# Opening by channel tiles and the end by halves of the tokens, in a two-layer decoder trunk

## The chip, the cores and the metric

The kernel runs on one core of a Trainium2 chip. TensorE (PE) multiplies matrices into PSUM banks, VectorE (DVE), ScalarE (ACT) and GpSimd (POOL) do the elementwise work, and the queues of SyncE (SP), ACT and POOL issue the DMA transfers. The metric is the device time of one execution in microseconds (us), lower is better. A profile is one execution with every instruction timed; its span is the time from the first to the last event on the core.

## The reference

One sequence of 256 tokens, 2048 channels, all in float32, two layers. Each layer has a token mixer and an MLP, and each of these is preceded by an RMSNorm with scale and shift computed from a vector `c` and followed by a gated residual:

```
mod = (silu(c) @ w_mod[i] + b_mod[i]);  sh1, sc1, g1, sh2, sc2, g2 = split(mod, 6)
u = rmsnorm(h, norm_mix_g[i]) * (1 + sc1) + sh1
h = h + g1 * mixer(u)          # layer 0: conformer convolution, layer 1: Mamba-2
u = rmsnorm(h, norm_mlp_g[i]) * (1 + sc2) + sh2
h = h + g2 * ((relu(u @ w1[i]) ** 2) @ w2[i])
return rmsnorm(h, final_norm_g)
```

The convolution mixer is `u @ w_pw1` (2048 to 4096 columns), a gated linear unit (GLU), a causal depthwise convolution of width 31, a LayerNorm with swish, and a second matrix. The Mamba-2 mixer projects to `z, x, B, C, dt`, convolves x, B and C over 4 positions, and scans over two chunks of 128 tokens in 8 groups of 8 heads: inside a chunk `(C B^T * decay) x`, across the chunks `C state * exp(acum)`, where `acum` is the running sum of `dt * A` in a chunk and `A = -exp(a_log)`. It ends with `y * silu(z)`, an RMSNorm per group, and an output matrix. The kernel must return the whole trunk's output.

## The kernel before

Activations lie with channels on partitions: `h[g]` holds four channel tiles of 128 channels by 256 tokens. Weights are read from HBM once each, in tiles of 1 MB (128 x 2048 float32). Large products split each weight tile into a high and a low half (`wh`, `wl`) by a cast on ACT and a difference on DVE, three or fewer products each; the first matrix of the convolution mixer is multiplied as it is.

*Modulation.* One segment (scale, shift, gate) of one channel tile is a product of a 1 MB tile of `w_mod` with `silu(c)`, held on all partitions in `scb`: one DVE instruction (L309) that also sums. `gemv` issues the load and this product, `mod_done` adds the bias and, for a scale, turns it into `(1 + scale) * norm gain`. The tiles rotate through four buffers `hid` and two `wm`. Modulation that is not needed at once is queued in `jobs` and pumped in between the weight tiles of later stages.

*The opening.* `conformer` squares x on ACT (L605, 16 instructions), sums over channels by 16 products with ones (L609), takes the root (L611). `native` then multiplies the first four blocks of 512 columns (`FIRST = 4`) of the first matrix; they fill all eight PSUM banks. It goes by groups of four channel tiles: all eight modulation products of group 0, the reciprocal of the root among them (L796), then four times a factor and a shift (`vectors`, L631 on DVE, L634 on ACT) to make `u[0]`; then for each group 0 to 2 and each block i a weight tile of 1 MB (512 rows by 512 columns) and its products (L760), with two modulation products of the next group behind each block. In group 3 the products go in three parts, two channel tiles, one and one, over all blocks. `glu` takes a block's banks when the last channel tile is in. After this, `native` is called once for each of the blocks 4 to 7, with the depthwise convolution of finished channel tiles on ACT, DVE and (for eight of the tiles) PE in between, and queued modulation.

All the small parameters are one tensor `par`, 1186 columns of 128 partitions, loaded at the start on ACT's queue. The tap weights of the PE convolution (`quad`) are loaded on POOL's queue. Weights and modulation tiles are loaded on SP's queue in program order (`stream`, L364); an issue waits there until its buffer is free.

*The second mixer.* `scores` and `scan` are generators: a step of theirs is taken between products of the projection (`step`), strictly one generator after the other, and `lag(n)` lets n steps pass. For each group `scores` loads the broadcast decays (`ac_d`, two `acc` tiles, on POOL's queue), adds the mask, takes exponentials; `scan` makes the state and adds the part from outside the chunk: a tile `e2` of the factors `exp(acum)` is loaded from `eac_d` (L1335, POOL's queue) and multiplied by `C state` (L1341). `gated` multiplies by the gate (L1363), squares (L1365), adds up (L1366, L1367) and sums over channels on PE (L558 in `rstd_cols`), for the root and reciprocal.

*The end.* The last MLP works with tokens on partitions: `ht[q]` holds the 128 tokens of half q by 2048 channels. `block_t` multiplies a block of 512 output columns for both halves, alternating between them, and the second half's products end a few instructions after the first's. `into_rows` multiplies the bank by the gate row (L1101), adds it to `ht` (L1105), squares with a sum (L1106), and multiplies by the final gain (L1107). `run` then adds the four sums of each half (L1406), takes root and reciprocal for both halves (L1407, L1408), scales (L1413 on ACT, L1415 on DVE) and stores four pieces of 512 KB (L1416).

The order on each engine is set by a list scheduler from the program order, the priorities (`high_priority`) and the explicit `issue_after`; SP's loads keep program order.

## Time and profile before

| | |
|---|---|
| median of the runs | 2562.72 us (2562.64 to 2563.96) |
| profiled execution | 2561.61 us, span 2559.8 us |
| PE busy | 2518.8 us |
| first product of the opening | 36.54 us |
| block 4 begins | 152.04 us |
| last product begins | 2547.57 us |
| loads and stores | 664.85 MB, mean 260 GB/s |

The profiled execution is 1.1 us below the median; its time lies 1.8 us above its span. In the rows of the profile, a line such as L760 is one of the kernel before, an operand `u,w` names tiles without their numbers, and a matmul of full float32 shows as two records each of its loads and its products. The idle time of an engine matters only where the end waits for it.

### The profile page before, as it was taken

What the parts mean: (1) busy time and instruction counts of PE and PEld (TensorE: products, weight loads), DVE (VectorE), ACT (ScalarE), POOL (GpSimd) and SP (SyncE); (2) the same over time, 40 slices, a digit from 0 to 9 for tenths busy, and PEclk for the clock granted to TensorE, in tenths of its full rate; (3) what the DMA queues carried; (4) which work ended last, traced back from release to release, by engine and by line L of the source; (5) the groups of instructions that cost most, each with busy time, mean ns of one, the idle gap of its engine ahead of it and who ended that gap; (6) DMA issues with size and microseconds to landing.
All of it is one profiled execution on the core that took longest, in us unless ns stands there. A gap on an engine that the chain in (4) does not pass through costs nothing. (4 is left out here: it accounts for less than half of the span.)

```text
span 2559.8 us, 36983 instructions
## 1 busy us (share of the span) xinstructions
PE 2518.8 (98%) x14707; PEld 2175.6 (85%) x14707; DVE 1916.5 (75%) x2467; ACT 1312.7 (51%) x2011; POOL 146.9 (6%) x212
## 2 busy tenths in 40 slices
PE   6999999999999999999999999999999999999998
PEld 5888799988888888888888888888998888888886
DVE  6679688878879878888777778898975565565565
ACT  2068454544434434448677777744454443443443
POOL 0011000000000000001000000000001101001000
PEclk8999999999999999999999999999999999999999
DMA  9998789688888878856555455688765555555553
GB/s 404 381 326 305 286 341 361 258 333 316 310 334 315 326 291 342 322 216 227 194 186 177 169 193 193 243 310 313 311 247 190 190 195 186 193 192 189 195 187 142
DMA packets 94895, 664.85 MB, mean 260 GB/s; under 512 B 10977, under 2 KB 10977, under 8 KB 16769
## 3 DMA queue, kind: packets, MB, share of 16 engines
q1 hardware_dynamic: 89138, 643.87, 68.0%
q0 software_dynamic: 5152, 16.97, 2.3%
q8 instruction: 115, 1.88, 0.3%
q10 hardware_dynamic: 432, 1.66, 0.2%
q14 instruction: 58, 0.48, 0.1%
HBM read 657.02 MB, written 2.20 MB: 258 GB/s over the span
## 5 line engine op out<-in xcount | busy, mean ns | idle before, releaser
L380 DVE TENSOR_TENSOR wl<-w,wh 128x1024 fp32r<-128x1024 f32 x768 | 940.9, 1229 | 472.6 <-ACT wh L378 468.2
L378 ACT CAST wh<-w 128x1024 fp32r<-128x1024 f32 x768 | 808.2, 1053 | 935.4 <-PE mm L409 478.5
L409 PE MATMUL mm<-u,wh 128*128 128x512 f32 x3136 | 994.2, 398 | 0.2 <-ACT wh L378 0.2
L409 PEld LDWEIGHTS mm<-u,wl 128*128 128x128 f32 x3136 | 587.7, 188 | 138.6 <-DVE wl L380 1.1
L409 PE MATMUL mm<-u,wl 128*128 128x256 f32 x3136 | 617.9, 278 | 0.7 <-DVE wl L380 0.7
L409 PEld LDWEIGHTS mm<-u,wh 128*128 128x128 f32 x3136 | 479.9, 189 | 7.7 <-issue 4.2
L462 PE MATMUL mm<-wh,hid 128*128 128x512 f32 x896 | 350.7, 391 | 0.0
L464 PE MATMUL mm<-wh,hid 128*128 128x512 f32 x896 | 348.7, 389 | 0.0
L463 PE MATMUL mm<-wl,hid 128*128 128x512 f32 x896 | 348.6, 389 | 0.0
L309 DVE SCALAR_TENSOR_TENSOR wm<-wm,scb 128x2048 f32<-128x2048 f32 x133 | 303.9, 2285 | 17.9 <-DMA wm<-wmT 17.9
L393 PE MATMUL mm<-u,wh 128*128 128x256 f32 x1408 | 254.7, 284 | 0.9 <-DVE u L523 0.6
L393 PEld LDWEIGHTS mm<-u,wh 128*128 128x128 f32 x1408 | 219.2, 192 | 4.0 <-ACT u L519 1.3
L760 PE MATMUL mm<-u,w 128*128 128x256 f32 x864 | 191.9, 383 | 20.4 <-ACT u L634 20.4
L760 PEld LDWEIGHTS mm<-u,w 128*128 128x128 f32 x864 | 164.6, 192 | 46.9 <-ACT u L634 21.6
L393 PE MATMUL mm<-u,wl 128*128 128x256 f32 x704 | 198.0, 283 | 0.6 <-DVE wl L380 0.6
L462 PEld LDWEIGHTS mm<-wh,hid 128*128 128x128 f32 x896 | 168.2, 188 | 35.6 <-issue 1.0
L464 PEld LDWEIGHTS mm<-wh,hid 128*128 128x128 f32 x896 | 168.2, 188 | 35.4
L463 PEld LDWEIGHTS mm<-wl,hid 128*128 128x128 f32 x896 | 168.2, 188 | 35.0 <-issue 0.5
L409 PE MATMUL mm<-hid,wh 128*128 128x512 f32 x448 | 141.9, 398 | 0.3 <-DVE lo L511 0.3
L309 DVE SCALAR_TENSOR_TENSOR hid<-hid,scb 128x2048 f32<-128x2048 f32 x47 | 107.3, 2286 | 40.8 <-DMA hid<-wmT 40.7
L393 PEld LDWEIGHTS mm<-u,wl 128*128 128x128 f32 x704 | 134.6, 192 | 0.8 <-DVE wl L380 0.8
L409 PEld LDWEIGHTS mm<-hid,wl 128*128 128x128 f32 x448 | 84.2, 188 | 19.8
(263 smaller groups left out, 1967.7 us busy)
## 6 DMA issues: line engine op xcount, KB each, us to landing
w<-w SPq DMA_DIRECT2D x256, 1024.0 KB, 4.9
wm<-wmT SPq DMA_DIRECT2D x138, 1024.0 KB, 7.1
w<-win SPq DMA_DIRECT2D x80, 1024.0 KB, 4.9
hid<-wmT SPq DMA_DIRECT2D x54, 1024.0 KB, 10.9
w<-pw SPq DMA_DIRECT2D x46, 1024.0 KB, 7.3
w<-wout SPq DMA_DIRECT2D x32, 1024.0 KB, 7.0
acc<-ac_d POOLq DMA_DIRECT2D x16, 512.0 KB, 7.2
xpad<-u POOLq DMA_DIRECT2D x24, 131.5 KB, 8.2
```

The lines of the kernel that those rows point to most:

```text
L309: self.sum = nc.vector.scalar_tensor_tensor(out=w, in0=w, scalar=1.0, in1=self.scb, op0=ALU.mult, op1=ALU.mult, accum_out=m[:, i:i + 1]).ins
L378: nc.scalar.copy(out=wh, in_=w[:, s, :])
L380: nc.vector.tensor_tensor(out=wl, in0=w[:, s, :], in1=wh.bitcast(F32), op=ALU.subtract)
L393: self.pe = self.nc.tensor.matmul(out, lhsT=lhsT, rhs=rhs, skip_group_check=True, **kw).ins
L409: self.pe = self.nc.tensor.matmul(out, lhsT=lhsT, rhs=rhs, start=start and not lows, stop=stop and bool(lows), skip_group_check=True).ins
L462: mm(banks[q], lhsT=hi, rhs=wh[:, k, :], start=g == 0 and t == 0, stop=False)
L463: mm(banks[q], lhsT=hi, rhs=wl[:, k, :], start=False, stop=False)
L464: mm(banks[q], lhsT=lo, rhs=wh[:, k, :], start=False, stop=g == 3 and t == 3)
L760: self.pe = nc.tensor.matmul(o, lhsT=w[:, t, j * P:(j + 1) * P], rhs=u[g][:, t, :], start=g == 0 and t == 0 and j < 2, stop=g == 3 and t == 3,
```

## The change

*Opening by channel tiles.* The first four blocks' weights become an array `open` of their own, arranged by channel tile: one 1 MB tile has the 128 rows of one channel tile for all four blocks (128 x 4 x 512). A new function `opening` goes through the 16 channel tiles: scale product, factor, shift product, `u` of this tile, then 16 products for all four blocks. Bias and gain of each single column are added on DVE (one, the shift of tile 14, on POOL). The squares of x are taken as three 128x1024 instructions and four small ones, added on DVE, and summed by 6 products instead of 16. 16 products that only fill PE's time stand between these sums and the first channel tile (`FILL[0]` was 0). Of `par` only the first 272 columns are loaded at the start, the rest behind the last `open` tile on SP's queue; the first `quad` load is held until the shift of tile 14 is made. `native` keeps blocks 4 to 7. The exponential for `A` (`na`) is held until the last square before the second mixer.

*End by halves.* In the very last block of `block_t` the products of the last six channel tiles are held and then issued for the first half of the tokens and after it for the second. `finish(q)` ends each half on its own: the sums of the first three blocks are added early, root and reciprocal, the last block times gain and reciprocal in one instruction, the rest scaled on DVE and ACT, two stores.

*Second mixer.* `e2` gets a place of its own in `par` (the columns of the depthwise taps, no longer needed), and its load is issued at the start of `scan`. `lag` before group 0's mask is 5 steps and not 3; after the last addition of `scan` 1 step and not 2; in `gated` 3 steps and not 2 (4 for group 0, as before).

```diff
-FILL = 0, 3, 5, 6, 8
+FILL = 16, 3, 5, 6, 8
...
+        "open": np.ascontiguousarray(pw1[:, :FIRST * 512].reshape(NT, P, FIRST, 512)),
...
-        nc.scalar.dma_start(out=self.par, in_=a["par"])
+        nc.scalar.dma_start(out=self.par[:, :SOON], in_=a["par"][:, :SOON])
...
-        if (layer, seg, kg) in ((0, SC1, 3), (0, SH1, 3)):
-            nc.vector.tensor_add(m, m, b)
+        if layer == 0 and seg in (SC1, SH1):
+            late = (seg, 4 * kg + i0) == (SH1, NT - 2)
+            self.closed = (nc.gpsimd if late else nc.vector).tensor_tensor(out=m, in0=m, in1=b, op=ALU.add).ins
...
+                held += [(4 * g + 2 * i + k, wh, wl, k) for k in range(2)]
+                if by_half and (g == 2 and i == 1 or g == 3 and i == 0):
+                    continue
+                order = [(q, *v) for q in range(2) for v in held] if g == 3 and i == 1 else [
+                    (q, *v) for v in held for q in range(2)]
+                for v in order:
+                    three(*v)
+                held = []
...
+        def opening(done):
...
+            self.turn_over(banks[0][0][:, :P], FILL[0], self.pe)
+            for ct in range(NT):
+                g, t = divmod(ct, 4)
+                self.gemv(0, SC1, ct, ((t, t + 1),))
+                if ct == 0:
+                    self.gemv(0, SH1, ct, ((t, t + 1),))
+                    with self.tc.issue_after(self.sum):
+                        nc.vector.reciprocal(r, r)
+                m = self.t("nrm", [P, T], bufs=2)
+                nc.vector.scalar_tensor_tensor(
+                    out=m, in0=self.h[g][:, t, :], scalar=self.mod_tile(0, SC1, g)[:, t:t + 1],
+                    in1=r, op0=ALU.mult, op1=ALU.mult)
+                if ct:
+                    self.gemv(0, SH1, ct, ((t, t + 1),))
+                if ct == NT - 2:
+                    self.after_open = self.closed
+                nc.scalar.activation(out=u[g][:, t, :], in_=m, func=AF.Identity,
+                                     bias=self.mod_tile(0, SH1, g)[:, t:t + 1])
+                w = self.load_w(a["open"][ct])
+                for i in range(FIRST):
+                    for j in range(4) if ct < NT - 1 else (0, 2, 1, 3):
+                        o = banks[i][j % 2][:, (j // 2) * T:(j // 2 + 1) * T]
+                        self.pe = nc.tensor.matmul(o, lhsT=w[:, i, j * P:(j + 1) * P], rhs=u[g][:, t, :],
+                                                   start=ct == 0 and j < 2, stop=ct == NT - 1,
+                                                   skip_group_check=True).ins
+                        if ct == NT - 1 and j >= 2:
+                            done(2 * i + j - 2, banks[i][j - 2])
+            self.stream(self.par[:, SOON:], a["par"][:, SOON:])
...
+    def finish(self, q):
+
+        nc, out, ht = self.nc, self.out, self.ht[q]
+        with self.tc.high_priority(AHEAD_CHAIN):
+            r = self.t("rcol", [P, 2])[:, :1]
+            nc.scalar.activation(out=r, in_=self.sq_row[:, q, 3:], func=AF.Sqrt, scale=1.0 / D, bias=self.part[q])
+            nc.vector.reciprocal(r, r)
+            nc.vector.scalar_tensor_tensor(out=ht[:, 1536:], in0=ht[:, 1536:], scalar=r, in1=self.fg_row[3],
+                                           op0=ALU.mult, op1=ALU.mult)
+            nc.vector.tensor_scalar_mul(out=ht[:, 1024:1536], in0=ht[:, 1024:1536], scalar1=r)
+            nc.scalar.mul(out=ht[:, :1024], in_=ht[:, :1024], mul=r)
+            for i in (1, 0):
+                nc.sync.dma_start(out=out[q, :, i * 1024:(i + 1) * 1024], in_=ht[:, i * 1024:(i + 1) * 1024])
...
+        with self.tc.issue_after(self.sq):
+            nc.scalar.activation(out=na, in_=self.col("a_log", 0)[:H], func=AF.Exp)
...
-            yield from lag(3)
+            yield from lag(5)
...
+        e2 = self.par[:, OFF["w_dw"]:OFF["w_dw"] + 4 * Q].rearrange("p (j l) -> p j l", j=4)
...
-        e2 = self.t("t2", [P, 4, Q], bufs=3)
...
-        yield from lag(2)
+        yield
...
-        yield from lag(2 if g else 4)
+        yield from lag(3 if g else 4)
```

What the scheduler makes of it at three places. First SP's queue from the first modulation tile on; `wmT` is the modulation matrix, `pw` the first matrix by blocks, `open` the same by channel tiles. Before:

```order
L364 DMA hid_203<-wmT 128x2048
L364 DMA hid_207<-wmT 128x2048
L364 DMA wm_211<-wmT 128x2048
L364 DMA hid_214<-wmT 128x2048
L364 DMA hid_218<-wmT 128x2048
L364 DMA wm_221<-wmT 128x2048
L364 DMA hid_224<-wmT 128x2048
L364 DMA hid_230<-wmT 128x2048
L364 DMA w_46_246<-pw 128x2048
```

Now:

```order
L367 DMA hid_205<-wmT 128x2048
L367 DMA hid_211<-wmT 128x2048
L367 DMA w_38_220<-open 128x2048
L367 DMA wm_238<-wmT 128x2048
L367 DMA hid_245<-wmT 128x2048
L367 DMA w_42_250<-open 128x2048
L367 DMA hid_268<-wmT 128x2048
L367 DMA wm_275<-wmT 128x2048
L367 DMA w_46_280<-open 128x2048
```

The first weight tile stood ninth and stands third now, and every third tile is one of weights.

The same place on DVE, from the first product with `scb` to the first factors `nrm`. Before:

```order
L309 SCALAR_TENSOR_TENSOR hid_203,mod_205<-hid_203,scb 128x2048
L309 SCALAR_TENSOR_TENSOR hid_207,mod_209<-hid_207,scb 128x2048
L309 SCALAR_TENSOR_TENSOR wm_211,mod_205<-wm_211,scb 128x2048
L309 SCALAR_TENSOR_TENSOR hid_214,mod_209<-hid_214,scb 128x2048
L796 RECIPROCAL t_16_160<-t_16_160 128x256
L309 SCALAR_TENSOR_TENSOR hid_218,mod_205<-hid_218,scb 128x2048
L309 SCALAR_TENSOR_TENSOR wm_221,mod_209<-wm_221,scb 128x2048
L309 SCALAR_TENSOR_TENSOR hid_224,mod_205<-hid_224,scb 128x2048
L631 SCALAR_TENSOR_TENSOR nrm_234<-h_75,mod_205,t_16_160 128x256
```

Now:

```order
L618 TENSOR_TENSOR acc_124<-acc_124,acc_126 128x1024
L618 TENSOR_TENSOR acc_124<-acc_124,acc_129 128x1024
L622 TENSOR_TENSOR acc_124<-acc_124 128x512
L311 SCALAR_TENSOR_TENSOR hid_205,mod_207<-hid_205,scb 128x2048
L336 TENSOR_TENSOR mod_207<-mod_207,par 128x1
L338 SCALAR_TENSOR_TENSOR mod_207<-mod_207,par 128x1
L311 SCALAR_TENSOR_TENSOR hid_211,mod_213<-hid_211,scb 128x2048
L765 RECIPROCAL t_17_146<-t_17_146 128x256
L336 TENSOR_TENSOR mod_213<-mod_213,par 128x1
L767 SCALAR_TENSOR_TENSOR nrm_217<-h_75,mod_207,t_17_146 128x256
```

Three additions of the squares stand ahead of the first product, and two products instead of seven ahead of the first factor.

Last, DVE at the very end, behind the last difference of a split (`wl`). Before:

```order
L1101 TENSOR_TENSOR t_3436_22132<-mm_22000,h_17493 128x512
L1105 TENSOR_TENSOR wm_17161<-wm_17161,t_3436_22132 128x512
L1101 TENSOR_TENSOR t_3437_22143<-mm_22001,h_17493 128x512
L1105 TENSOR_TENSOR wm_17162<-wm_17162,t_3437_22143 128x512
L1107 TENSOR_TENSOR wm_17161<-wm_17161,h_17582 128x512
L1107 TENSOR_TENSOR wm_17162<-wm_17162,h_17582 128x512
L1406 TENSOR_REDUCE rcol_22148<-mom_16271 128x2
L1408 RECIPROCAL rcol_22148<-rcol_22148 128x2
L1415 TENSOR_SCALAR wm_17161<-wm_17161,rcol_22148 128x1024 x2
```

Now:

```order
L1102 TENSOR_TENSOR t_3431_22148<-mm_22028,h_17515 128x512
L1106 TENSOR_TENSOR wm_17183<-wm_17183,t_3431_22148 128x512
L1124 RECIPROCAL rcol_22152<-rcol_22152 128x1
L1125 SCALAR_TENSOR_TENSOR wm_17183<-wm_17183,rcol_22152,h_17604 128x512
L1127 TENSOR_SCALAR wm_17183<-wm_17183,rcol_22152 128x512
L1102 TENSOR_TENSOR t_3433_22178<-mm_22029,h_17515 128x512
L1106 TENSOR_TENSOR wm_17184<-wm_17184,t_3433_22178 128x512
L1124 RECIPROCAL rcol_22182<-rcol_22182 128x1
L1125 SCALAR_TENSOR_TENSOR wm_17184<-wm_17184,rcol_22182,h_17604 128x512
L1127 TENSOR_SCALAR wm_17184<-wm_17184,rcol_22182 128x512
```

The first half's whole chain (tile `wm_17183`) now stands ahead of the second half's first instruction; before, the halves went in turns and shared the reciprocal.

More of the change, by code (lines that the diff above doesn't have):

```diff
@@ L674, in weigh @@
             if queue:
-                queue.dma_start(out=w, in_=src)
+                with self.tc.issue_after(self.after_open):
+                    queue.dma_start(out=w, in_=src)
             else:
```

191 lines of the change are left out of this document (77 added, 114 removed).

## The prediction

> **What bounds the kernel now.** The table of engines comes first. TensorE (PE) is busy nearly all of the 2559.8 us, so a change can win only where PE waits, runs slowly, or has finished.
>
> ```profile
> PE 2518.8 (98%) x14707; PEld 2175.6 (85%) x14707; DVE 1916.5 (75%) x2467; ACT 1312.7 (51%) x2011; POOL 146.9 (6%) x212
> PE mm L760 <- ACT u L634: 20.4, 3, 17.9
> PE ms L558 <- DVE wm L1367: 1.6, 2, 1.1
> DVE t L1341 <- DMA t<-eac_d: 18.4, 6, 6.0
> ```
>
> The last three rows are from the list of waits: who waited for whom, total, times, longest. PE's one large wait is in the opening. The short waits at L558 and the 18.4 us for which VectorE (DVE) sits before L1341 belong to the second mixer.
>
> Next, the opening in stretches. Columns: PE, weight loads, DVE, ScalarE (ACT) and POOL busy, then granted clock, DMA share, GB/s.
>
> ```profile
> 36.50:59.50 23.00, 22.96 (x98) 19.94 (x99) 14.51 (x14) 1.30 (x3) 0.00 (x0) 0.91 1.01 420
> 59.50:110.00 50.50, 48.05 (x222) 41.56 (x221) 35.98 (x39) 3.65 (x8) 1.59 (x8) 1.00 1.01 419
> 110.00:130.00 20.00, 20.00 (x94) 17.62 (x93) 5.97 (x11) 1.42 (x3) 0.00 (x0) 1.00 0.77 297
> 130.00:152.00 22.00, 22.00 (x103) 19.36 (x103) 10.77 (x16) 6.82 (x14) 1.85 (x4) 1.00 0.69 277
> 152.00:200.00 48.00, 48.00 (x316) 39.30 (x316) 43.25 (x51) 43.91 (x110) 7.27 (x13) 1.00 1.01 342
> 200.00:260.00 60.00, 60.00 (x441) 47.55 (x440) 58.34 (x72) 45.14 (x113) 8.19 (x15) 1.00 0.85 304
> ```
>
> Up to 110 us the DMA engines are full at 420 GB/s. From 110 to 152 they idle 20 x 0.23 + 22 x 0.31 = 11.4 us while PE is full. So the opening is bound by DMA first and by PE afterwards. Had PE started sooner, it would have less left when the last weights are there. The timeline (start, length) gives the durations:
>
> ```profile
> 13.75 2.29 DVE L309 SCALAR_TENSOR_TENSOR hid<-hid,scb 128x2048 f32<-128x2048 f32 x1 [7.04 <-DMA hid<-wmT]
> 18.65 2.29 DVE L309 SCALAR_TENSOR_TENSOR wm<-wm,scb 128x2048 f32<-128x2048 f32 x1 [0.19 <-DMA wm<-wmT]
> 21.14 2.29 DVE L309 SCALAR_TENSOR_TENSOR hid<-hid,scb 128x2048 f32<-128x2048 f32 x1 [0.19 <-DMA hid<-wmT]
> 23.36 1.75 DVE L796 RECIPROCAL t<-t 128x256 f32<-128x256 f32 x1
> 35.98 0.91 ACT L634 ACTIVATE u<-nrm,mod 128x256 f32<-128x256 f32 x2 [15.52 <-POOL mod L337]
> 36.54 22.89 PE L760 MATMUL mm<-u,w 128*128 128x256 f32 x96 [17.94 <-ACT u L634]
> 96.68 20.99 PE L760 MATMUL mm<-u,w 128*128 128x256 f32 x96 [2.02 <-ACT u L634]
> 104.44 2.29 DVE L309 SCALAR_TENSOR_TENSOR wm<-wm,scb 128x2048 f32<-128x2048 f32 x1 [2.47 <-DMA wm<-wmT]
> 108.05 2.28 DVE L309 SCALAR_TENSOR_TENSOR hid<-hid,scb 128x2048 f32<-128x2048 f32 x1
> 110.57 0.91 ACT L634 ACTIVATE u<-nrm,mod 128x256 f32<-128x256 f32 x2 [12.47 <-DVE mod L333]
> 152.04 7.07 PE L760 MATMUL mm<-u,hid 128*128 128x256 f32 x32
> 158.95 7.07 PE L760 MATMUL mm<-u,w 128*128 128x256 f32 x32
> ```
>
> PE stands for 17.94 us until the first `u`, starts at 36.54 us, and ends the four opening blocks at 152.04 us, where block 4 (its weights in `hid`) begins. 32 records, which are 16 products of 128x256, take 158.95 - 152.04 = 6.91 us. Two products of L309 that wait only for the next 1 MB tile start 21.14 - 18.65 = 2.49 us apart: the DMA price of a tile, and 1.05 MB at 420 GB/s says the same.
>
> **The opening, part by part.** It needs 32 modulation tiles and 16 MB of weights, 48 tiles of 1 MB, before and after. The change reads them as two modulation tiles and one weight tile per channel tile, so after 3 tiles PE can work on 16 products.
>
> *Start.* The first product of L309 waited until 13.75 us for its tile. Ahead of it lay x, all of `par` (0.61 MB) and a `quad` tile (0.52 MB); now 0.14 MB of `par` and no `quad`, so it lands 0.99 MB / 420 GB/s = 2.4 us sooner, near 11.4 us. Two products instead of eight stand ahead of the first `u`. From 13.75 us, if DVE is no sooner free of the three new additions: two products (2.4 each), the reciprocal 1.75, some 1.5 for small operations, `u` 0.5, which makes 22 us; from 11.4 us it is 19.6. The 16 filling products of 128 columns lie in that wait; at twice the price they would cost PE 3 us, which the sum below does not feel.
>
> *Pace.* A channel tile costs DMA 3 x 2.49 = 7.47 us and PE 6.91 us. DVE and ACT need 110.57 - 104.44 = 6.13 us from the first product's start to `u`'s, below 7.47. PE alone would end at 22 + 16 x 6.91 = 132.6 us, so DMA sets the end.
>
> *End.* Tile 48 lands at 11.4 + 47 x 2.49 = 128.4 us. The `quad` load, now held until the vectors are nearly done, shares the engines there: 0.52 MB, 1.25 us, 129.7 us. The last scale tile lands two tiles ahead of that, at 124.7 us; then 6.13 to the last `u`'s start, 0.56 to PE (36.54 - 35.98), 6.91 of products: 138.3 us. (The rows: the load of `par`, all DMA of the first 130 us, and the decay loads of the second mixer, which come up below.)
>
> ```profile
> par<-par ACTq DMA_DIRECT2D x1, 593.0 KB, 4.0
> DMA packets 7422, 51.07 MB, mean 393 GB/s; under 512 B 817, under 2 KB 817, under 8 KB 1585
> acc<-ac_d POOLq DMA_DIRECT2D x16, 512.0 KB, 7.2
> ```
>
> Against 152.04 us that is **13.7 us** sooner. Bounds: without the `quad` 15.0; at the mean of the first 130 us, idle DMA time included (the second row below), a tile costs 2.67 us, 45 x 0.18 = 8.1 us more, so 5.6. I take 13.7, since 73 us of rows show 420 GB/s for this very mix of tiles. Slots don't bind: a weight slot frees when PE is done three channel tiles before, some 13 us ahead of need, and the queue needs 2.5 us per tile.
>
> [...]
>
> *After the opening* blocks 4 to 7 follow in the same order on PE. They move 13.7 us ahead if their weights do: block 4's first tile is three tiles behind tile 48 (0.47 MB of `par`, then itself), at about 133 us, and it is needed at 138.3. The rest of `par` lands by 131 us and the depthwise convolution's first use of it is after the first GLU, 1.7 us into the last channel tile (133 us).
>
> **The end.** Start, length; DMA's second row gives GB/s in 40 slices of 2545 to 2560 us:
>
> ```profile
> 2547.34 0.39 PE L463 MATMUL mm<-wl,hid 128*128 128x512 f32 x1
> 2547.57 0.39 PE L464 MATMUL mm<-wh,hid 128*128 128x512 f32 x1
> 2548.00 0.69 DVE L1101 TENSOR_TENSOR t<-mm,h 128x512 f32<-128x512 f32 x1
> 2548.72 0.69 DVE L1105 TENSOR_TENSOR wm<-wm,t 128x512 f32<-128x512 f32 x1
> 2549.45 0.63 ACT L1106 ACTIVATE t<-wm 128x512 f32<-128x512 f32 x1 [0.64 <-DVE wm L1105]
> 2550.20 0.69 DVE L1107 TENSOR_TENSOR wm<-wm,h 128x512 f32<-128x512 f32 x1 [0.19 <-ACT t L1106]
> 2551.00 0.29 ACT L1407 ACTIVATE rcol<-rcol,eps 128x2 f32<-128x2 f32 x1 [0.83 <-DVE rcol L1406]
> 2551.53 2.19 ACT L1413 ACTIVATE wm<-wm,rcol 128x1024 f32<-128x1024 f32 x2 [0.23 <-DVE rcol L1408]
> 2551.53 1.42 DVE L1415 TENSOR_SCALAR wm<-wm,rcol 128x1024 f32<-128x1024 f32 x2
> GB/s 0 0 0 0 0 0 0 0 0 0 0 0 0 0 0 0 0 0 0 0 0 131 382 415 415 393 382 415 404 415 415 404 404 404 415 197 0 0 0 0
> ```
>
> Now: PE ends at 2547.96, the scaling begins at 2551.53, the first quarter is scaled at 2552.24, bytes flow from 2552.9 to 2558.2 (2.1 MB at 405 GB/s), the span ends 1.6 us later. After: the same 2548.00 to 2550.20 for the second half's product, addition and square, then at once root and reciprocal (2551.53 - 2551.00 = 0.53), then 1.10 for the longest scaling: 2551.83. Bytes 0.66 later, but 1.05 MB: 2.6 us, then 1.6, which makes 2556.7. **3.1 us** less. The cover of the first half: it is done 18 products earlier, 18 x 0.23 = 4.1 us of PE, its own chain takes 0.72 + 0.73 + 0.75 + 0.53 + 1.10 = 3.83 and so frees DVE and ACT before the second begins; its 2.6 us of bytes end ahead of 2552.5. If that cover is gone, up to 1 us. The split of the last weights waits for the slot of the piece consumed when the held six channel tiles begin; 12 products of the first half (2.7 us) cover its cast and difference (about 2.4). Bounds 2 to 4.
>
> **The second mixer.** `e2`, which made DVE sit 18.4 us (six times), is requested a whole scan earlier in a buffer of its own, so those gaps close. Most cost PE nothing: PE stood only at L558, 1.6 us there, because the gated sum of squares came late. With the gaps gone and the gated product one place earlier, I take 1.6. Neither end is excluded: L558 itself is also placed up to four rows of products earlier (0.7 us each time for two groups), and POOL's queue, in order, now holds `e2` for group g+1 ahead of decays for group g+1 to g+2 (loss to 2 us if these come late; the `acc<-ac_d` row above shows 7.2 us to land and they are needed some 20 us after the previous scan's end). The exponential of `a_log` moves behind the second mixer's first root and brings its table load there:
>
> ```profile
> 5.03 1.28 ACT L1231 ACT_TABLE_LOAD   x1
> 6.32 0.20 ACT L1231 ACTIVATE na<-par 64x1 f32<-64x1 f32 x1
> 1134.45 0.91 ACT L522 ACTIVATE u<-nrm,mod 128x256 fp32r<-128x256 f32 x2 [1.34 <-DVE nrm L592]
> ```
>
> 1.48 us where ACT idles 1.34: 0.2 lost. Net **1.4 us**, between a loss of 2 and a gain of 3.
>
> **Sum.** 13.7 + 3.1 + 1.4 = 18.2. The profiled span becomes 2541.6, that execution 2561.61 - 18.2 = 2543.4. The median of the runs shown, 2562.72, is 1.1 above that execution; from it 2544.5 us.
>
> **Rivals.** *Given back in blocks 4 to 7.* DVE is busy 58.34 of 60 us from 200 to 260, ACT 43.91 of 48 before. DVE now starts this stretch with one modulation product (2.2 us) not yet done that it had done at 145 us, and DMA has no idle time left behind it. If DVE paces the stretch, 2 to 5 us come back: about 2548. Against it: PE shows no wait there, so there is slack of unknown size.
>
> *Slower: DMA falls to 342 GB/s*, as from 152 to 200 us with the engines equally full. A tile costs 3.07 us; the opening ends at 11.4 + 45 x 3.07 + 1.5 + 13.6 = 164.7, 12.7 late, less 4.5: 2570.9. It decides from 2.90 us per tile, 362 GB/s: there 45 x 2.90 + 26.5 = 157 us equals the gain elsewhere. Against it: that stretch carries small copies between partitions, the opening none. [...]
>
> *PE's clock.* Each channel tile leaves PE a gap of 0.56 us. At half clock a tile is 13.8 us and the opening 91 us longer. But the gap of 2.02 us before 96.68 left the clock at 1.00, so 0.56 will. [...]
>
> *The change doesn't do what it says:* slots hold the queue as they do from 110 us now, and the 11.4 us of idle DMA remain: 2555.9. *Or only the opening gains* and the other two terms vanish: 2549.
>
> **Chances.** Forecast 0.66 (2541 to 2548 its own range); given back 0.16; only the opening 0.09; idle DMA remains 0.05; slower 0.04. Range 2540 to 2552: the bounds of the opening (5.6 to 15.0), the end and the mixer, with the first rival and the case in which only the opening gains. No change means within 0.2%, 5.1 us, about what a measurement of this kernel can tell. Faster 0.94, same 0.02, slower 0.04.
>
> **What would show it.** Opening: PE from about 22 us, DMA share 1.0 until 128 us, gaps of half a microsecond between channel tiles from the sixth on, block 4 near 138 us; later than 143 refutes the pace. Blocks 4 to 7: PE without new waits and the last of them 13 to 14 us sooner; else the first rival. End: output in two bursts and 8.7 us from the last product to the span's end instead of 11.8. Mixer: no wait for `eac_d` on DVE, none at the gated sums on PE. The prediction is wrong if PE gains waits behind DVE or DMA outside these places.

## The result, and the profile after

| | before | after |
|---|---|---|
| median of the runs | 2562.68 us (2560.65 to 2563.96) | 2549.24 us (2547.76 to 2550.19) |
| ratio | | 0.9948, 95% interval 0.9931 to 0.9965 |
| profiled execution, span | 2561.61, 2559.8 us | 2549.99, 2548.2 us |

The change saves 13.4 us. Forecast were 2544.5 us, 18.2 us saved, in a range of 2540 to 2552. So sign and range were right, and 4.8 us are missing from the sum; the time is outside the narrower 2541 to 2548 that the forecast itself was given. Both profiles have the same marks on PE: the start of block 4, the sums of the norms (L558 before, L568 now), the end of the last product.

| mark on PE | before, us | after, us | sooner |
|---|---|---|---|
| block 4 begins | 152.04 | 138.28 | 13.76 |
| norm ahead of the first MLP | 409.56 | 395.22 | 14.34 |
| norm ahead of the second mixer | 1130.03 | 1117.32 | 12.71 |
| norm ahead of the last MLP | 1827.86 | 1818.94 | 8.92 |
| last product ends | 2547.96 | 2539.06 | 8.90 |
| span | 2559.8 | 2548.2 | 11.6 |

The opening came as forecast (13.8 us for 13.7), the end nearly so (2.7 us for 3.1). The second mixer, forecast to gain 1.4 us, lost 3.8, and 1.6 us went between the first MLP's norm and the second mixer. The list of waits of the changed kernel (who waited for whom: total, times, longest) has one large row of PE that was not there before:

```profile
DVE acc L1320 <- DMA acc<-ac_d: 5.3, 2, 3.5
PE mm L412 <- DVE xpad L1167: 4.3, 1, 4.3
PE mm L780 <- ACT u L774: 4.2, 12, 0.7
```

The last row is the opening: 12 gaps, 4.2 us in all, in place of 20.4 us in three waits, the longest 17.9. The first two are new. Its timeline shows the place, the first group of the second mixer (POOL issues the decay loads, DVE adds the mask, L1320):

```profile
1164.90 0.58 POOL L1284 DMA_DIRECT2D ac_d<-wm  x1 [55.86 <-DVE wm L1274]
1167.40 0.54 POOL L1285 DMA_DIRECT2D eac_d<-wm  x1 [1.93 <-ACT wm L1281]
1168.85 1.83 POOL L1314 DMA_DIRECT2D acc<-ac_d  x2 [0.91 <-DMA ac_d<-wm]
...
1172.45 0.48 DVE L1187 SCALAR_TENSOR_TENSOR a<-xpad,par,a 128x256 f32<-128x256 f32 x1
1176.40 1.23 DVE L1320 TENSOR_TENSOR acc<-acc,mask 128x1024 f32<-128x1024 f32 x1 [3.47 <-DMA acc<-ac_d]
1179.50 1.23 DVE L1320 TENSOR_TENSOR acc<-acc,mask 128x1024 f32<-128x1024 f32 x1 [1.88 <-DMA acc<-ac_d]
1180.65 1.22 DVE L383 TENSOR_TENSOR wl<-w,wh 128x1024 fp32r<-128x1024 f32 x1
1181.78 0.42 DVE L1167 TENSOR_TENSOR xpad<-mm,lo 128x256 f32<-128x256 f32 x1
...
1182.25 1.22 PE L412 MATMUL mm<-u,wh 128*128 128x512 f32 x2 [4.31 <-DVE xpad L1167]
```

The same place before:

```profile
1181.84 0.93 POOL L1291 DMA_DIRECT2D acc<-ac_d  x1 [2.91 <-DMA ac_d<-wm]
1182.76 0.55 POOL L1262 DMA_DIRECT2D eac_d<-wm  x1
...
1188.97 1.22 DVE L1297 TENSOR_TENSOR acc<-acc,mask 128x1024 f32<-128x1024 f32 x1
1190.11 0.42 DVE L1145 TENSOR_TENSOR xpad<-mm,lo 128x256 f32<-128x256 f32 x1
1190.48 1.23 DVE L380 TENSOR_TENSOR wl<-w,wh 128x1024 fp32r<-128x1024 f32 x1
1191.62 0.42 DVE L1145 TENSOR_TENSOR xpad<-mm,lo 128x256 f32<-128x256 f32 x1
1191.96 1.22 DVE L1297 TENSOR_TENSOR acc<-acc,mask 128x1024 f32<-128x1024 f32 x1
```

Two things are different, and both are order. On POOL's queue the write of `eac_d`, which waits for ACT, now stands ahead of the first decay load. On DVE both masks stand together, ahead of a cast difference and of the two additions into `xpad` that free PE's banks; before, the second mask stood behind them. Before, 7.1 us lay between the issue of the first load (1181.84) and the first mask's turn (1188.97); now 4.1 (1168.85 to 1172.93, the end of L1187). The time to land changed too. This is the first decay load alone, before and after (size, us from issue to landing):

```profile
acc<-ac_d POOLq DMA_DIRECT2D x1, 512.0 KB, 4.5
acc<-ac_d POOLq DMA_DIRECT2D x1, 512.0 KB, 7.5
```

Counted from the norm ahead of the second mixer, the load is issued no later than before (51.5 us behind it, 51.8 before). But it lands at 59.1 us instead of 56.3, and the mask's turn comes at 55.6 instead of 58.9. By these times either shift alone would have made a wait of 0.7 us at most; together they make 3.5. Of the later landing the traces show only how it stands beside the order on POOL's queue: 7.5 us here and 7.4 in the kernel before with `na` late (below; 1182.01 to the first mask at 1189.42, which waited for it), both with `eac_d` ahead, against 4.5 in the kernel before, with `eac_d` behind the first load. DVE waits 3.47 and 1.88 us with everything behind it, and PE waits 4.31.

The granted clock (the number after POOL's, then DMA share and GB/s) shows that this is not all:

```profile
395.15:398.56 3.41, 3.30 (x29) 2.32 (x26) 2.25 (x4) 1.86 (x4) 0.00 (x0) 1.00 0.81 262
398.56:401.97 3.41, 3.41 (x18) 0.59 (x16) 3.21 (x7) 0.91 (x2) 0.00 (x0) 0.50 0.73 240
1177.00:1182.00 5.00, 0.94 (x7) 0.65 (x5) 3.12 (x4) 1.60 (x3) 0.00 (x0) 0.82 1.04 254
1182.00:1184.00 2.00, 1.75 (x5) 1.56 (x6) 1.99 (x4) 1.77 (x7) 0.00 (x0) 0.50 1.03 289
1184.00:1186.00 2.00, 2.00 (x7) 1.61 (x7) 0.42 (x1) 0.63 (x3) 0.00 (x0) 0.50 1.04 369
1186.00:1188.00 2.00, 2.00 (x11) 1.75 (x10) 0.85 (x1) 1.91 (x3) 0.00 (x0) 0.74 0.54 221
```

After the wait PE runs at half clock from 1182 to about 1187 us. Taken by the clock alone this adds 4 x 0.5 + 2 x 0.26 = 2.5 us, an estimate; four products of L412 take 1.28 us there (1183.70 to 1184.98) and 0.70 behind it (1187.32 to 1188.02). The second row is another stretch, without a wait, at which the 1.6 us between the first MLP and the second mixer went; it comes up again at the end.

### The profile page after: what moved, and what is told of

Same layout as the page of the kernel before. It is cut to its first block, busy times and chain, and to the rows that moved or that the text cites. A ratio compares the mean times of both kernels' runs of the same rounds, so it can differ in the third digit from the quotient of the medians.

```text
span 2548.2 us, 37057 instructions
## 1 busy us (share of the span) xinstructions
PE 2523.3 (99%) x14719; PEld 2174.8 (85%) x14719; DVE 1928.4 (76%) x2512; ACT 1316.6 (52%) x2008; POOL 147.5 (6%) x201
## 3 DMA queue, kind: packets, MB, share of 16 engines
q8 instruction: 115, 1.88, 0.3%
## 4 chain that ended last, share of the span: by engine, by line
PE 94%; DMA 3%; DVE 2%; ACT 1%; issue 0%; SPq 0%; POOL 0%; DVEq 0%; ACTq 0%
PE mm L412 49%; PE mm L396 11%; PE mm L454 8%; PE mm L455 8%; PE mm L456 8%; PE mm L810 4%; DMA hid<-wmT 1%; PE mm L719 1%; PE mm L780 1%; PE ms L1373 1%; DMA wm<-wmT 1%; DMA w<-open 1%; DVE hid L311 0%; DMA acc<-ac_d 0%; PE ms L780 0%; PE ms L302 0%
## 5 line engine op out<-in xcount | busy, mean ns | idle before, releaser
L412 PE MATMUL mm<-u,wh 128*128 128x512 f32 x3136 | 996.3, 399 | 4.5 <-DVE xpad L1167 4.3
L412 PEld LDWEIGHTS mm<-u,wl 128*128 128x128 f32 x3136 | 588.7, 188 | 139.2 <-DVE wl L383 1.1
L412 PE MATMUL mm<-u,wl 128*128 128x256 f32 x3136 | 617.7, 279 | 0.6 <-DVE wl L383 0.6
L412 PEld LDWEIGHTS mm<-u,wh 128*128 128x128 f32 x3136 | 480.6, 189 | 12.6 <-issue 4.9
L412 PE MATMUL mm<-hid,wh 128*128 128x512 f32 x448 | 141.9, 398 | 0.0
L311 DVE SCALAR_TENSOR_TENSOR hid<-hid,scb 128x2048 f32<-128x2048 f32 x47 | 107.3, 2286 | 20.4 <-DMA hid<-wmT 20.4
L810 PE MATMUL mm<-u,w 128*128 128x256 f32 x480 | 105.8, 381 | 0.0
L810 PEld LDWEIGHTS mm<-u,w 128*128 128x128 f32 x480 | 90.6, 190 | 14.9 <-issue 2.9
L412 PEld LDWEIGHTS mm<-hid,wl 128*128 128x128 f32 x448 | 84.1, 188 | 19.7
```

Of the source, the lines that this page charges most:

```text
L311: self.sum = nc.vector.scalar_tensor_tensor(out=w, in0=w, scalar=1.0, in1=self.scb, op0=ALU.mult, op1=ALU.mult, accum_out=m[:, i:i + 1]).ins
L412: self.pe = self.nc.tensor.matmul(out, lhsT=lhsT, rhs=rhs, start=start and not lows, stop=stop and bool(lows), skip_group_check=True).ins
L810: self.pe = nc.tensor.matmul(o, lhsT=w[:, t, j * P:(j + 1) * P], rhs=u[g][:, t, :], start=g == 0 and t == 0 and j < 2, stop=g == 3 and t == 3,
```

## The experiments

Each was run beside the kernel before, four to eleven executions, and the ratio is to that. "Changed" is the changed kernel, 2549.24 us. The kernel before had medians of 2561.35, 2562.12 and 2562.27 us in the three batches, so less than a microsecond between two runs tells nothing.

| run | median, us | ratio to before, 95% interval |
|---|---|---|
| changed, `na` at the start | 2542.26 | 0.9926 (0.9914 to 0.9939) |
| changed, `na` behind `e` | 2541.71 | 0.9920 (0.9908 to 0.9933) |
| before, `na` late | 2569.93 | 1.0032 (1.0020 to 1.0043) |
| changed, `e2` late | 2554.82 | 0.9975 (0.9966 to 0.9984) |
| changed, masks held | 2545.49 | 0.9939 (0.9927 to 0.9952) |
| changed, mixer as before | 2543.20 | 0.9932 (0.9919 to 0.9944) |
| `na` at the start, `e2` late | 2549.57 | 0.9949 (0.9935 to 0.9962) |
| `na` at the start, lags as before | 2544.14 | 0.9927 (0.9914 to 0.9939) |
| `na` behind `e`, end as before | 2545.40 | 0.9935 (0.9922 to 0.9947) |
| `na` behind `e`, one tile more | 2546.46 | 0.9934 (0.9922 to 0.9947) |
| `na` behind `e`, four tiles fewer | 2536.48 | 0.9899 (0.9884 to 0.9914) |
| `na` behind `e`, no filling | 2542.20 | 0.9920 (0.9908 to 0.9933) |

### Which edit made the wait

Theory A: the late exponential of `a_log` (`na`). Theory B: the early load of `e2`, which shares POOL's queue with the decays. Theory C: the decays are late whatever the order. First `na` alone is undone; its column moves into the first part of `par`.

```diff
-        with self.tc.issue_after(self.sq):
-            nc.scalar.activation(out=na, in_=self.col("a_log", 0)[:H], func=AF.Exp)
+        nc.scalar.activation(out=na, in_=self.col("a_log", 0)[:H], func=AF.Exp)
```

> The changed kernel with one thing undone: the exponential of a_log (na) is computed at the start again (its column is loaded with the first part of par). Theory A (the late na shifts the chain to the decays, and by that the order: eac_d is written ahead of the first decay load, and both masks of group 0 stand together ahead of a cast difference and two additions into xpad that PE waits for): the two masks stand apart again, PE's wait of 4.31 us at L412 and the 1.9 us at half clock behind it vanish, less up to 1.3 us for table loads at the start: 2543 to 2544.5 us. Theory B (the e2 load on POOL's queue delays the decays) and theory C (the decays collide with a 1 MB weight tile whatever the order): no change, 2548 to 2550 us, wait of 3 us or more still there.

Measured: 2542.26 us, 7.0 less than the changed kernel. The masks stand apart again and the wait is gone, which speaks against theories B and C. Block 4 begins at 138.66 us, 0.4 later; the table loads at the start are not shown to be the reason, for two of the runs below that also have `na` at the start begin it at 138.3.

The counter-proof is the same edit, made the other way, in the kernel before:

```diff
-        nc.scalar.activation(out=na, in_=self.col("a_log", 0)[:H], func=AF.Exp)
+        with self.tc.issue_after(self.sq):
+            nc.scalar.activation(out=na, in_=self.col("a_log", 0)[:H], func=AF.Exp)
```

> The kernel before with one edit of the change: na held behind the last square before the second mixer. Theory A: the late na alone makes the wait: the two masks stand together, PE waits 3.5 to 4.5 us behind them and runs 3.5 us at half clock; 4.5 to 6.5 us slower than before, less up to 1 us that the missing table load may give at the start: 2565 to 2568 us. Rival (the wait needs the opening's shift or e2's new place): within 1 us of before, 2560.5 to 2562.5 us.

Measured: 2569.93 us, 7.8 slower than before, more than expected. Its timeline, waits and clock (rows in the same columns as above):

```profile
1189.42 1.23 DVE L1298 TENSOR_TENSOR acc<-acc,mask 128x1024 f32<-128x1024 f32 x1 [3.47 <-DMA acc<-ac_d]
1191.71 1.22 DVE L1298 TENSOR_TENSOR acc<-acc,mask 128x1024 f32<-128x1024 f32 x1 [1.06 <-DMA acc<-ac_d]
...
PE mm L409 <- DVE xpad L1145: 3.5, 1, 3.5
PE ms L558 <- DVE wm L1368: 3.1, 2, 2.0
...
1194.50:1198.00 3.50, 3.50 (x12) 3.03 (x13) 2.12 (x4) 1.60 (x6) 0.00 (x0) 0.58 1.03 357
1239.00:1243.00 4.00, 4.00 (x16) 3.42 (x17) 2.05 (x5) 1.39 (x2) 0.00 (x0) 0.65 0.94 338
```

The wait is there without the new opening and without `e2`'s new place. The rest of the 7.8 us is a second wait in the same group, at its gated sums (L558, 2.0 us at 1236), and a second stretch at half clock behind it. One instruction of 0.2 us, moved, costs a third of a per cent.

Is it that `na` is late, or what its table load does to the order? `na` can stay late if it goes behind the exponential `e` of the time steps, for which the table is loaded anyway:

```diff
-        nc.scalar.activation(out=e, in_=e, func=AF.Exp)
+        behind = nc.scalar.activation(out=e, in_=e, func=AF.Exp).ins
...
-        with self.tc.issue_after(self.sq):
+        with self.tc.issue_after(behind):
             nc.scalar.activation(out=na, in_=self.col("a_log", 0)[:H], func=AF.Exp)
```

> The changed kernel; na is not held behind the last square before the second mixer but behind the exponential e of the time steps, which needs the same table, so that no table load is added or moved. Theory A (what hurts is the order that follows from the moved table load, not that na is late): the two masks of group 0 stand apart as with na at the start, no wait at group 0, and the opening is 0.4 us sooner than with na at the start (138.3 instead of 138.66 us): 2541 to 2542.5 us. Rival (na late in itself delays the chain to the decays): 2545 us or more with a wait of 2 us or more at L412 near 1177 us.

Measured: 2541.71 us, the fastest that computes the whole trunk, and faster than both kernels: 0.9920 of before, 7.5 us below the changed one. Its timeline at the place of the wait:

```profile
1167.07 0.94 POOL L1314 DMA_DIRECT2D acc<-ac_d  x1 [2.68 <-ACT wm L1281]
1168.00 0.55 POOL L1285 DMA_DIRECT2D eac_d<-wm  x1
...
1174.42 1.22 DVE L1320 TENSOR_TENSOR acc<-acc,mask 128x1024 f32<-128x1024 f32 x1
1177.41 1.21 DVE L1320 TENSOR_TENSOR acc<-acc,mask 128x1024 f32<-128x1024 f32 x1
```

The first decay load is ahead of `eac_d` again, 7.35 us lie between its issue and the first mask, and the mask does not wait for it. So a late `na` does no harm by itself. What differs is the place of the table load, 1.28 us at 1119.48 us in the changed kernel and 1146.22 here, and the order that the scheduler makes of the 60 us behind it. Why the scheduler makes this order of it was not tried.

Next, order against landing. Here only the masks of group 0 are held behind the last issued addition into `xpad`:

```diff
-            with self.tc.issue_after(c["mark"]):
+            with self.tc.issue_after(c["mark"] if g else self.xadd):
```

> The changed kernel, na late and e2 early as changed; only the masks of group 0 may not be taken before the last addition into xpad that the program has issued, which puts the second mask behind two cast differences and two additions instead of ahead of them, and the first mask one cast difference sooner. Theory A: DVE still waits for the first decay tile (some 3 to 4 us) but for the second no longer ahead of PE's banks: PE's wait falls from 4.31 us to 0.5 to 2.5 us and its clock stays up: 2544 to 2547 us. Theory C (the landing of the decays alone decides): the first mask alone holds the cast difference as long, wait 3 us or more, 2548 to 2550 us.

```profile
1177.07 1.23 DVE L1320 TENSOR_TENSOR acc<-acc,mask 128x1024 f32<-128x1024 f32 x1 [5.53 <-DMA acc<-ac_d]
...
PE mm L412 <- DVE wl L383: 2.9, 2, 2.2
```

Measured: 2545.49 us, 3.7 less than changed. DVE waits as long as before in all (5.5 us, for the first tile now), but with less behind it, so PE's wait falls from 4.3 to 2.2 us; the clock did not stay up, it is 0.61 from 1181 to 1185. Landing and order both count: late tiles cost what is queued behind their first reader. (This run's profile also has the stretch at half clock near 400 us: 0.58 from 398.5 to 402.)

Last, `e2` late again in its old place, `na` late:

```diff
-        e2 = self.par[:, OFF["w_dw"]:OFF["w_dw"] + 4 * Q].rearrange("p (j l) -> p j l", j=4)
-        for f in range(2):
-            src = self.eac_d[h0:h0 + 8, :].rearrange("(j f) l -> f j l", f=2)[f:f + 1]
-            nc.gpsimd.dma_start(out=e2[64 * f:64 * f + 64], in_=src.broadcast_to([64, 4, Q]))
         yield
...
         nc.scalar.copy(out=state, in_=sp)
+        e2 = self.t("t2", [P, 4, Q], bufs=3)
+        for f in range(2):
+            src = self.eac_d[h0:h0 + 8, :].rearrange("(j f) l -> f j l", f=2)[f:f + 1]
+            nc.gpsimd.dma_start(out=e2[64 * f:64 * f + 64], in_=src.broadcast_to([64, 4, Q]))
```

> The changed kernel with e2 loaded late and in its old place (one of three t2 buffers); lags and na as changed. Theory A: the masks still stand together, so the wait of some 4 us at group 0 stays, and DVE sits again before L1341's counterpart, which costs PE little: 2549 to 2552 us. Theory B: POOL's queue has no e2 behind the decays, they land about 1 us sooner, PE's wait at group 0 falls below 1 us: 2543 to 2545 us. Theory C: 2548 to 2550 us.

Measured: 2554.82 us, slower than theory A had it. The wait at group 0 stays (3.4 us), which ends theory B, and PE waits 5.7 us more at the gated sums, since DVE sits 24.9 us before the product with `e2`. That led to the next question.

### What the second mixer's own edits are worth

Three runs have `na` at the start. The first has `e2` late, as in the diff above. The second has the lags as before:

```diff
-            yield from lag(5)
+            yield from lag(3)
...
         nc.vector.tensor_add(x[:, :, Q:], x[:, :, Q:], e2)
-        yield
+        yield from lag(2)
...
-        yield from lag(3 if g else 4)
+        yield from lag(2 if g else 4)
```

The third has both, which makes the mixer that of the kernel before.

> The changed kernel with na at the start and e2 loaded late into t2, lags as changed. Against the run with na at the start alone (2542.3 us) this prices e2's place. Theory D (with the new lags the late e2 makes the gated sums late, as in the run with e2 late, where PE waited 5.7 us at them): 2546 to 2548.5 us, DVE sitting 20 us or more before the product with e2. Rival (those waits came from the masks of group 0 and the shift they left): 2542.5 to 2544 us.

> The changed kernel with na at the start and the three lags as before (3, 2, 2), e2 early. Against the run with na at the start alone (2542.3 us) this prices the lags. If the lags matter by themselves, the gated sums are multiplied up to 0.7 us earlier in the program and PE waits at them 0.5 to 1.5 us in all: 2543 to 2544 us. If only e2's place matters: 2542 to 2542.6 us.

> Opening and end as changed, the second mixer wholly as before (e2 late in t2, lags 3, 2, 2, na at the start). The changed kernel's profile gives 13.8 us for the opening and 2.7 us for the end, and 4.9 us lost in the second mixer. Theory A: that loss goes with na, and the mixer's stalls of 1.6 us at the gated sums come back: 2562.7 - 16.5 = 2546.2 us, 1 to 2 us above the run with na early. Theories B and C: B gives the same 2546; C 2549 to 2551 us. The prediction's own sum (13.7 and 3.1) gives 2545.9 us.

With the run that has only `na` undone, the medians make a table of two by two:

| | lags changed | lags as before |
|---|---|---|
| `e2` early | 2542.26 | 2544.14 |
| `e2` late | 2549.57 | 2543.20 |

The changed lags with a late `e2` are 7.3 us slower, a microsecond more than theory D had it: DVE waits for the factor, the gated sum is late, PE waits for it, and the mean clock is 0.997, against 0.999 with `e2` early. From that run's waits:

```profile
DVE t L1363 <- DMA t<-eac_d: 23.3, 8, 6.5
PE ms L568 <- DVE wm L1389: 4.1, 2, 2.9
```

With `e2` early neither wait is there, in either column. The two edits together are worth 0.9 us by the medians (2543.20 to 2542.26) and 0.8 by the marks around the mixer, against 1.6 in the forecast's sum; the executions of the two runs overlap, so this is not clear of noise. The run with `e2` early and the lags as before has no wait in the mixer either; its profile has the stretch at half clock near 400 us (0.58 from 398.5 to 402), 1.6 us, which that of the run with only `na` undone has not (1.00 there), so its 1.9 us cannot be put down to the lags.

One thing stays open. With the mixer wholly as before, the second mixer still runs 1.9 us faster than in the kernel before (1115.97 to 1811.95 us, against 1130.03 to 1827.86). PE's waits account for most of it: 3.9 us in seven gaps before, 2.4 in five here, and 1.2 us of the difference lie at the gated sums (2.07 before, 0.91 here). Why these waits are shorter when only the time ahead of the mixer has changed is not settled.

### The opening's bound

One more load of 1 MB, into a buffer that nobody reads:

```diff
+                if ct == 6:
+                    self.load_w(a["open"][ct])
                 w = self.load_w(a["open"][ct])
```

> The kernel with na behind e (2541.7 us) with one more load of 1 MB between the loads of the opening (channel tile 6's weights are loaded twice, once into a buffer that nobody reads). If the DMA engines set the pace of the opening from the fourth channel tile on, block 4 begins 2.5 us later (140.8 instead of 138.3 us) and the time is 2544.2 us. If PE, DVE or ACT set it, block 4 begins within 0.6 us of 138.3 and the time stays within 1 us.

Four modulation tiles fewer, which leaves the shift out of `u` for these channel tiles, so that the output is another:

```diff
-                if ct:
+                if ct and not 6 <= ct < 10:
                     self.gemv(0, SH1, ct, ((t, t + 1),))
```

> The kernel with na behind e (2541.7 us) without the shift of channel tiles 6 to 9: four modulation tiles of 1 MB and their four products on DVE are left out, and u of these tiles has no shift (the output changes). If DMA alone set the pace, block 4 would begin 10 us sooner, at 128.3 us. PE's own bound: 6.91 us per channel tile without the gaps of 0.57 us from tile 6 on, 10 gaps, 5.7 us sooner: 132.6 us, 2536.0 us. I expect the second, which is the prediction's figure for PE alone. If DVE or ACT were the bound, the gaps would stay and the gain be under 3 us.

The PE timelines, first of the run with one tile more, then of the one with four fewer:

```profile
65.41 5.42 PE L782 MATMUL mm<-u,w 128*128 128x256 f32 x24 [1.61 <-DMA w<-open]
74.09 5.45 PE L782 MATMUL mm<-u,w 128*128 128x256 f32 x24 [1.53 <-ACT u L774]
81.57 5.45 PE L782 MATMUL mm<-u,w 128*128 128x256 f32 x24 [0.30 <-ACT u L774]
...
141.02 1.24 PE L812 MATMUL mm<-u,hid 128*128 128x256 f32 x5
```

```profile
77.08 5.34 PE L780 MATMUL mm<-u,w 128*128 128x256 f32 x24
83.98 5.34 PE L780 MATMUL mm<-u,w 128*128 128x256 f32 x24
...
132.33 4.05 PE L810 MATMUL mm<-u,hid 128*128 128x256 f32 x18
```

One tile more moves block 4 from 138.36 to 141.02 us: 2.66 us, and no later gap makes it up. The other runs with the opening as changed begin block 4 between 138.3 and 139.2 us, so the 2.66 are good to about a microsecond, which is enough to tell it from the 0.6 us of the other case. DMA sets the pace. (The median is 4.75 us higher; the remaining 2 us are mostly the stretch at half clock near 400 us, which this run's profile has (0.89 from 398.5 to 402, 0.62 from there to 405.5) and that of the kernel with `na` behind `e` has not (1.00).) Four tiles fewer bring 6.0 us and not 10: the gaps are gone, channel tiles follow each other every 6.90 us, and PE is the bound, at 132.33 us where the forecast had PE alone at 132.6. That the two are so close is in part luck: PE starts at 19.23 us here and not at the forecast's 22, and the gaps that are left up to the sixth channel tile make up for it. The time is 2536.48 us, 2536.0 expected.

```diff
-FILL = 16, 3, 5, 6, 8
+FILL = 1, 3, 5, 6, 8
```

> The kernel with na behind e (2541.7 us) with 1 filling product instead of 16 ahead of the first channel tile. PE then idles some 3.5 us longer before it starts; its clock may fall to half for the first products, as in the kernel before (36.5 to 40.4 us). If DMA sets the opening's pace, a start that is slower by 2 to 4 us is hidden by the gaps of 0.57 us that follow, and block 4 begins at 138.3 us, 2541 to 2542.5 us. If not, 1.5 to 3.5 us slower.

```profile
20.17 6.98 PE L780 MATMUL mm<-u,w 128*128 128x256 f32 x24 [3.19 <-ACT u L774]
...
138.23 2.11 PE L810 MATMUL mm<-u,hid 128*128 128x256 f32 x9
```

Without the filling PE waits 3.2 us, the mean clock from 15 to 24 us is 0.81, and the first 24 records take 6.98 us instead of 5.38. Block 4 begins at 138.23 us all the same, against 138.36 with the filling. Here a slow start was free; the filling products, 3.85 us of PE in the changed kernel at clock 1.00 where the prediction had 3 at twice the price, bought nothing.

### The end

```diff
-                if by_half and (g == 2 and i == 1 or g == 3 and i == 0):
-                    continue
...
-            elif b == 3:
-                self.finish(q)
...
+        r = self.t("rcol", [P, 2])
+        nc.vector.reduce_sum(out=r, in_=self.sq_row, axis=mybir.AxisListType.X)
```

Behind these two lines stands the old end with its root, scaling and stores.

> The kernel with na behind e (2541.7 us) with its end as before: the last products in turns between the halves, both halves finished together, four pieces scaled and stored at the end. By the profiles the end takes 11.84 us from the last product to the span's end before and 9.15 us now: 2.7 us slower, 2544.4 us. The prediction's sum: 3.1 us, 2544.8. Rival (what the end by halves gains is paid for by the split and the order of the last products ahead of it): within 1 us, 2541 to 2542.7 us.

Measured: 2545.40 us, 3.7 slower; from the last product's end to the span's end it is 12.5 us (2533.38 to 2545.85), against 9.15 with the end by halves. That is 3.3 us, and by the profiles the edit's worth lies between this and the 2.7 of the two first profiles.

## Why the prediction was right or wrong

**Opening: right in its mechanism.** The changed kernel's timeline, and its stretches:

```profile
11.27 2.29 DVE L311 SCALAR_TENSOR_TENSOR hid<-hid,scb 128x2048 f32<-128x2048 f32 x1 [0.58 <-DMA hid<-wmT]
19.72 5.38 PE L780 MATMUL mm<-u,w 128*128 128x256 f32 x24
41.38 5.45 PE L780 MATMUL mm<-u,w 128*128 128x256 f32 x24 [0.74 <-ACT u L774]
124.89 2.29 DVE L311 SCALAR_TENSOR_TENSOR hid<-hid,scb 128x2048 f32<-128x2048 f32 x1 [1.99 <-DMA hid<-wmT]
130.61 0.51 ACT L774 ACTIVATE u<-nrm,mod 128x256 f32<-128x256 f32 x1 [6.90 <-DVE mod L336]
138.28 7.07 PE L810 MATMUL mm<-u,hid 128*128 128x256 f32 x32
...
59.50:110.00 50.50, 48.34 (x217) 40.34 (x216) 36.43 (x57) 3.55 (x7) 0.00 (x0) 1.00 1.01 420
110.00:130.00 20.00, 19.30 (x89) 16.36 (x88) 15.63 (x21) 1.02 (x2) 0.87 (x2) 1.00 1.01 416
138.30:200.00 61.70, 61.70 (x427) 49.86 (x426) 60.22 (x71) 54.85 (x139) 12.25 (x20) 1.00 0.98 331
```

First tile 11.27 us (forecast 11.4), PE from 19.72 (19.6, or 22 if DVE were not free; the signs named 22), last scale tile 124.89 (124.7), block 4 at 138.28 (138.3). As PE started sooner, the gaps came from the fourth channel tile on, not the sixth. The terms listed for the start add up to 22.3 and 19.95 us and not to 22 and 19.6, which changes nothing, since DMA sets the end. DMA moved 416 to 420 GB/s all the way; the rival at 342 GB/s did not come. *Given back in blocks 4 to 7* did not come either, with DVE at 60.2 of 61.7 us: PE has no wait above 0.3 us from block 4 to the norm behind them, and at that norm it is 14.34 us ahead, 0.6 more than at block 4.

**End: right, 0.4 us too good.** Measured 9.15 us for 8.7. The chain of the second half was right (3.87 forecast, 2539.06 to 2542.98 is 3.92). Short were the 4.9 us behind it: from there to the span's end it is 5.2.

**Second mixer: the edit that I priced at 0.2 us cost 6.6.** The step that failed is "1.48 us where ACT idles 1.34: 0.2 lost". At its own place the moved instruction cost no more than that: PE's wait at the mixer's start is 0.69 us, 0.62 before, and the table load is not one more but the one for `e` (1.28 us at 1160.57 before), moved ahead to 1119.48. But this also changed the scheduler's order 50 us on, and I had costed the moved instruction by its own length alone. Both consequences stood in the order of instructions: the write of `eac_d` ahead of the first decay load on POOL's queue, and the two masks of group 0 together on DVE. The prediction had a row for it (`acc<-ac_d`, 7.2 us to land, the median of 16 loads; this first one took 4.5) and named late decays as a loss of up to 2 us, but placed them behind `e2` at groups 1 and later, where there were none. Group 0, where the load can be issued only when the running sums are made and is needed at once, it did not price. The loss of up to 2 us that the bounds allowed was also too small, because half clock came with PE's wait of 4.31 us (0.50 from 1180.21 to 1187.04 us). From the norm ahead of the second mixer to the one ahead of the last MLP, the changed kernel loses 3.8 us; with `na` behind `e` it gains 2.8 (1115.73 to 1810.75 us): 6.6 for this edit. The other part of the step held: DVE's 18.4 us before `e2` and PE's 1.6 at L558 are gone from the list.

**The sum.** Of the 18.2 us, the second mixer took 5.2 (3.8 lost for 1.4 gained), the stretch at half clock near 400 us 1.6, the end 0.4; 0.7 came from the opening and blocks 4 to 7. That is 11.7, measured 11.6 by the spans. Freed of the late table load, the change gives 20.4 us (2562.12 to 2541.71), more than the sum.

**Luck.** The range held, but not for its reasons: the mixer came out below its own bound (3.8 us lost, 2 allowed), and the range had room for that only because it was made wide for the opening's lower bound and for two rivals. The time, 2549.24 us, is just that of the rival *only the opening gains* (2549), yet its condition did not come: the end gained 2.7 us, and the mixer did not come to nothing but lost.

## What to carry to other kernels

When a list scheduler sets the order, price a moved instruction by what stands in another order afterwards, not only by its length: compare the order of the queues that issue loads, and for each load that is needed soon, the time from its issue to its reader's turn with the time that it takes to land, which was not the same in the two orders (4.5 us before, 7.5 now). Among the places to look at, take first the one with the least such time, here the first group. Where a table load must be moved, put the function behind another that needs the same table (here 2541.71 us against 2549.24); and where DMA sets the pace, count megabytes and leave the compute side alone (1 MB more moved block 4 by 2.66 us, a start without the filling left it at 138.23, from 138.36).

## What the runs showed of the hardware

Some waits of PE had half clock behind them. After 4.31 us (changed kernel) the granted clock was 0.50 until 1187.04 us, for 4.79 us of PE's work, which by the clock alone is 2.4 us on top, an estimate; after 2.2 us (masks held) it was 0.61 over 4 us; after 2.0 us (`na` late in the kernel before, at 1236 us) 0.65 over 4 us; yet the wait of 2.02 us in the opening before (1.00 from 95.03 to 98.44 us) and the gaps of 0.3 to 0.7 us in the opening now (1.00 from 40 to 130 us) left it at 1.00. So the length of the wait alone does not decide, as the prediction's argument on PE's clock had taken it to.

The traces of the two kernels also give the length of each stretch. In the changed kernel the clock is full for 382.29 us from 16.27 us on, half for 3.41, full for 778.24 and half for 6.83; in the kernel before it is half for 17.07 us from 23.36 us on, then full for 2512.21. These are 112, 1, 228, 2, 5 and 736 times 3.41 us. Counted in steps of this length from the changes on, the 2.02 us in the opening before are cut by a step's start, and 1.65 us of them lie in the step from 95.03 us, after which the clock stays; of the 4.31 us in the changed kernel 2.27 lie in the step from 1176.80 us, and the next step is at half. From 40 us to the last product no other step at full clock of these two traces has more than 1.13 us idle. Two cases don't show at which idle time the clock falls, and no run varied it.

The clock also fell without a wait: between 398.56 and 401.97 us PE is busy the whole time at clock 0.50 (the row in the first section). The 3.41 us ahead of it have 0.11 us idle, but are full of products of 32 output columns (L302) and sums of one column (L568). Of ten profiles read at this norm five have such a stretch, at a cost of 1.6 us by the marks of the changed kernel: that kernel (0.51 from 398.5 to 402), masks held and lags as before (0.58), the end as before (0.66) and one tile more (0.62 from 402 to 405.5). The other five ran the same norm at 1.00. What tells the ones from the others is not shown; no run moved the norm alone. The stretch may also make much of the spread of 2.4 us among the executions of the changed kernel: two have a mean clock of 0.997, and the other two, done 1.5 to 2.4 us sooner, 0.998; only one of the four has a trace.
